# Smaller part tiles, and more products in pairs with a seven-product step, in a TensorE-bound decoder layer

## The chip, the cores and the metric

One core of one Trainium2 chip runs the whole layer. The metric is device time in microseconds (us), the median over several executions. Every matmul streams 512 columns of 32-bit data unless said otherwise.

## The reference

One hybrid decoder layer for 256 tokens of width 2048, in 32-bit floating point:

```
hn = rmsnorm(x);  q, k, v, g_ret, xr, yr, g_a, g_b = split(hn @ w_in)
ret_out = silu(g_ret) * groupnorm(retention(rotary(q), rotary(k), v))
rnn_out = gelu(yr) * rg_lru(causal_conv(xr))
merged  = sigmoid(g_a) * (ret_out @ w_proj_ret) + sigmoid(g_b) * (rnn_out @ w_proj_rnn)
h  = x + merged @ w_mix_out
h += cross_attention(rmsnorm(h), rmsnorm(mem))           # 256 memory tokens, 4 heads
up = causal_conv3(rmsnorm(h) @ ffn_w_up)                 # 2048 -> 2 * 5632
h += (silu(gate half of up) * value half) @ ffn_w_down
out = rmsnorm(h)
```

## The kernel before, in words

**Products.** An operand is kept as two parts, `hi` (rounded to the matmul's input format) and `lo` (what is left), and each product of two tiles is three matmuls: hi by hi, lo by hi, hi by lo. The activation side is stationary (128 x 128), the weight side streams (128 x 512). All large products are cut in column blocks of 512 (`BW`) and in k tiles of 128; the 256 tokens are two tiles of rows.

**Singles.** `gemm_n` (by `steps_n`) does one column block: it goes through its chunks of four k tiles (`KC`), and each chunk is 2 x 4 x 3 = 24 matmuls into one PSUM tile `acc` (three buffers of two banks).

**Pairs.** `pair` (by `steps_pair`) does two column blocks together. A chunk is a pair of k tiles (`KH`) of both blocks, also 24 matmuls, so a pair of 16 k tiles has eight chunks. At the k-pairs listed in `SEVEN` the four tile products of a 2 x 2 by 2 x 2 block product are replaced by Winograd's form with seven: 21 matmuls. It needs sums of the four weight tiles (four additions on the raw weights, L350), which are then split into parts like the weights themselves (`seven_parts`, seven part tiles instead of four), and sums of the activations (`sums_of`, kept in `token_sums`). It also needs four more PSUM banks, which are read into two SBUF tiles `o1`, `o2` after the last such k-pair (L495 to L502); at the pair's end four more additions (L513) bring in the other four banks.

**Weights.** `weight_plan` is the order of all products, `weight_stream` the order of their chunks in memory. A chunk of 1 MB is loaded to a `raw` tile (three buffers), ACT casts it to `hi` and the DVE subtracts to get `lo`. `prefetch` keeps two chunks prepared ahead of the one in use (`AHEAD = 2`); `hi` and `lo` have three buffers of 8 KB per partition (`PART_BUFS`).

**Order of the rest.** `chunks` counts a step after every chunk. `later(n, fn)` puts a piece of work into the program `n + 1` steps on. `by_dma` copies a result's 16-bit halves to planes on ACT (L535), transposes them by two DMAs on SP's queue (L536), and `wait + 1` steps later `join` puts them together on ACT (L548) and calls what follows. Every piece of work has its place in program order as its priority; an engine's queue is filled ahead of time from what is ready by an estimate, earlier place first, so a later piece can slip in while an earlier one isn't ready. The matmuls keep program order. Work in `high_priority(FREE)` is moved 300 places up. All tiles of 4 KB per partition share 29 buffers.

**The stages that the change touches**, in order: queries, keys, values and gates of retention (two groups of heads `g`), singles; `retain(g)` runs in small steps between the next products. Then the recurrence's blocks (singles), the gates `O_GB` (four singles), then `w_proj_rnn`, `O_GA` and `w_proj_ret`, two pairs each. In `w_mix_out` blocks 0 and 1 are a pair and blocks 2 and 3 singles; its left side `merged` is made by `turn_merged` from the joined results of `w_proj_ret`, block by block, two k-pairs from each. While it runs, `memory_steps` lets ACT take the squares of the rows of `mem` (L623), whose load is issued after the transposes. In the feed-forward, `ffn_w_up` runs as 22 singles, gate block and value block in turn; `conv_up` scales a result by the row norm on the DVE (L561), turns it by `by_dma` and applies three taps (L1107, L1109); after the value half `gate_up` forms `silu(gate) * value` (L1127 to L1129, L571, L572). After each of the first two parts of four blocks stands a `down` of two pairs, after the third `down_final`.

Of the kernel before, what the change touches and what calls it, by code (L numbers as in the profile page):

```python
# [17 lines left out]
P = 128  # L18
# [14 lines left out]
PART_BUFS = 3  # L33
# [9 lines left out]
SEVEN_O = (3, 5)  # L43

# [22 lines left out]

def weight_plan():

    plan = []  # L70
    for g in range(2):
        for c in (O_Q, O_K):
            plan += [("w_in", 0, NT, c + g * BW), ("w_in", 0, NT, O_V + g * 1024 + (c == O_K) * BW)]
        plan += [("w_in", 0, NT, O_G + g * 1024 + b * BW) for b in range(2)]
    for b in range(4):
        plan += [("w_in", 0, NT, c + b * BW) for c in (O_XR, O_YR)]
    plan += [("w_in", 0, NT, O_GB + b * BW) for b in range(4)]
    for w, c in (("w_proj_rnn", 0), ("w_in", O_GA), ("w_proj_ret", 0)):
        plan += [(w, 0, NT, (c + b * BW, c + (b + 1) * BW, SEVEN)) for b in (0, 2)]
    plan += [("w_mix_out", 0, NT, (0, BW, SEVEN))] + [("w_mix_out", 0, NT, b * BW) for b in (2, 3)]  # L80
    plan += [(w, 0, NT, b * BW) for b in range(4) for w in ("xa_w_k", "xa_w_q")]
    plan += [("xa_w_v", 0, NT, b * BW) for b in range(4)]
    plan += [("xa_w_o", 0, NT, (0, BW, SEVEN_O))] + [("xa_w_o", 0, NT, b * BW) for b in (2, 3)]
    for kind, *a in ff_plan():
        if kind == "down" and sum(a) < NF // 4:
            plan += [("ffn_w_down", a[0] * BW, 4 * a[1], (b * BW, (b + 1) * BW, SEVEN)) for b in (0, 2)]
        elif kind == "down":
            plan += [("ffn_w_down", a[0] * BW, 4 * a[1], b * BW) for b in range(4)]
        else:
            plan.append(("ffn_w_up", 0, NT, (0 if kind == "gate" else FF) + a[0] * BW))  # L90
    return plan
# [7 lines left out]
def ff_plan():  # L99

    out, b0 = [], 0
    for nb_ in FF_PARTS:
        ups = [(kind, b) for b in range(b0, b0 + nb_) for kind in ("gate", "value")]
# [47 lines left out]
def hybrid_layer(  # L151
# [104 lines left out]
    in_order = {sum(len(pieces(i, a[2], a[3])) for i, a in enumerate(plan[: gate_up_at() + 1])) + 1}  # L256

    def prefetch(n):
        while len(ahead) < n and taken[0] < len(stream):
# [56 lines left out]
            hi, lo = part_tiles()  # L316
            for k in range(0, nk, KH):
                if own:
                    xs[k2 + k // KH]
                if isinstance(c, tuple):  # L320
                    if k == 0:
                        weight_parts(raw, hi, lo)
                    continue
                for cs in (slice(k, k + 1), slice(k + 1, k + 2)) if i < 4 else (slice(k, k + KH),):
                    if i == 0 and cs.start == 0:
                        dve.tensor_copy(hi[:, cs], raw[:, cs, :])
                    else:
                        act.copy(hi[:, cs], raw[:, cs, :])  # L328
                    with tc.issue_after(split[cs.start]) if i == 0 else nullcontext():
                        dve.tensor_tensor(  # L330
                            out=lo[:, cs], in0=raw[:, cs, :], in1=hi[:, cs].bitcast(F32), op=ALU.subtract
                        )
            ahead.append(((row, c), (hi, lo)))

    def part_tiles():
        return [wp.tile([P, KC, BW], F32R, tag=a, bufs=PART_BUFS, name=nm(a)) for a in ("hi", "lo")]

    def weight_parts(src, hi, lo):

        act.copy(hi, src)  # L340
        dve.tensor_tensor(out=lo, in0=src, in1=hi.bitcast(F32), op=ALU.subtract)  # L341

    def seven_parts(raw):

        b12, b11, b22, b21 = (raw[:, i, :] for i in range(4))
        p_hi, p_lo = part_tiles()
        q_hi, q_lo = part_tiles()
        weight_parts(raw[:, 1:4], p_hi[:, 0:3], p_lo[:, 0:3])
        for o, a, b in ((b11, b12, b11), (b12, b12, b22), (b22, b11, b22), (b21, b22, b21)):
            dve.tensor_tensor(out=o, in0=a, in1=b, op=ALU.add)  # L350
        for c in (slice(0, 2), slice(2, 4)):
            weight_parts(raw[:, c], q_hi[:, c], q_lo[:, c])
        p1, p3, p2 = ((p_hi[:, i, :], p_lo[:, i, :]) for i in range(3))
        q3, q1, q2, q4 = ((q_hi[:, i, :], q_lo[:, i, :]) for i in range(4))
# [40 lines left out]
    def steps_n(w, row, st, nk, col):  # L395
# [3 lines left out]
        for k0, n, parts in chunks(nk, w, row, col):  # L399

            def tile_(tt, kk):
                k = k0 + kk
                hi, lo = (t[:, kk, :] for t in parts)
# [53 lines left out]
    def steps_pair(w, row, st, nk, c1, c2, seven=SEVEN):  # L457
# [14 lines left out]
        for k0, n, parts in chunks(nk, w, row, (c1, c2, seven)):  # L472
# [30 lines left out]
            else:  # L503
                end = k0 + n == nk
                for b, names in enumerate((("p2", "p4"), ("x3", "n"))):
                    hi, lo = (t[:, b * KH : (b + 1) * KH, :] for t in parts)
                    for tt, name in enumerate(names):
                        for j in range(KH):
                            rows_of(name, own[tt][j], (hi[:, j, :], lo[:, j, :]), end and j == KH - 1)
# [286 lines left out]
    for g in range(2):  # L796
        dec = big([P, 4, S], s="dec")
        vs, turned = [], ([], [])
        for b, o in enumerate((O_Q, O_K)):
# [12 lines left out]
            v = gemm_n("w_in", 0, xs, NT, O_V + g * 1024 + b * BW) if g + b else ended(v_steps)  # L812
            vs.append(split_rows(v, rs0))
        qr, kr = turned
        gates = []
        for b in range(2):
            a = gemm_n("w_in", 0, xs, NT, O_G + g * 1024 + b * BW)
# [3 lines left out]
            dve.scalar_tensor_tensor(out=t, in0=t, scalar=1.0, in1=a, op0=ALU.add, op1=ALU.mult)  # L821
            gates.append(t)
# [136 lines left out]
    ts = [tanh_rows(big([P, 2, BW], s="sig"), gemm_n("w_in", 0, xs, NT, O_GB + b * BW)) for b in range(4)]  # L959
    mb = []  # L960
    for b in (0, 2):
        for i, z in enumerate(pair("w_proj_rnn", 0, rnn, NT, b * BW, (b + 1) * BW)):
            gated(ts[b + i], z)
# [17 lines left out]
    def residual(w, st, out, wcol, steps=None):  # L981

        ss = sums()
        sources = []
        for b in range(4):
            if steps:
                steps(b)
            if not sources:
                if b == 0:
                    sources += pair(w, 0, st, NT, b * BW, (b + 1) * BW, SEVEN if steps else SEVEN_O)  # L990
                else:
                    sources.append(gemm_n(w, 0, st, NT, b * BW))
            h = hrow[b]
            dve.tensor_add(h, h, sources.pop(0))
# [119 lines left out]
    def conv_up(c0, b, dst, then):  # L1114


        def turned(f):
            conv(f, c0 // P + 4 * b, dst)
            then()

        turned_rows(gemm_n("ffn_w_up", 0, h2s, NT, c0 + b * BW), rs2, turned)

# [36 lines left out]
    def last_down(b0, hid, n, b):  # L1159
# [5 lines left out]
        parts = [p for _, _, p in chunks(n, "ffn_w_down", b0 * BW, b * BW)]  # L1165

        def total(o, tt, cs):
            for k in range(n):
                hi, lo = (t[:, k % KC, cs] for t in parts[k // KC])
# [50 lines left out]
    hid, gts = {}, {}  # L1220
    for kind, b, *n in ff_plan():
        if kind == "gate":
            gts[b] = big([P, 4, S], s="fg")
            conv_up(0, b, gts[b], lambda: None)
        elif kind == "value":
            vl = big([P, 4, S], s="fv")
            b0 = max(one[1] for one in ff_plan() if one[0] == "down" and one[1] <= b)
            seven = tuple(i - 2 * (b - b0) for i in SEVEN) if b0 < sum(FF_PARTS[:2]) else ()
            conv_up(FF, b, vl, lambda b=b, vl=vl, n=seven: gate_up(gts[b], vl, hid.setdefault(b, []), n))
# [50 lines left out]
```

## Time and profile before

| | before |
|---|---|
| median of 3 runs (lowest to highest) | 2017.43 us (2016.87 to 2017.99) |
| profiled execution | 2015.44 us |
| its span, first to last instruction | 2013.6 us |
| mean granted TensorE clock | 0.995 |
| TensorE matmul (PE) busy | 1985.5 us, 99% |
| VectorE (DVE) busy | 1450.8 us, 72% |
| ScalarE (ACT) busy | 1295.0 us, 64% |
| DMA | 425.54 MB, mean 211 GB/s |

In the profile's lines PE is TensorE's matmuls and PEld its weight loads, SPq is the queue of DMA issues on SyncE. A matmul's shown length is modelled and overlaps the next one's, so the pace is read from the starts. `x2` counts merged instructions; a bracket holds the engine's idle time before the instruction and what ended it. `acc` and `sm` are PSUM tiles, `s` and `ts` parts of activations and of their sums.

### The profile page before, as it was taken

Reading aid. Unit: us, or ns where it says so; the run is one execution under the profiler, and the core shown is the slowest. Engines: PE = TensorE matmul, PEld = TensorE weight load, DVE = VectorE, ACT = ScalarE, POOL = GpSimd, SP = SyncE. Lnnn points to the kernel's source line nnn. Section 1 sums busy time; section 2 is a strip of 40 time slices with the busy share of each in tenths; the row PEclk is TensorE's granted clock in tenths of the full one; section 3 lists DMA queues with packets and bytes.
Section 4 is the critical chain, followed back from the end, with each engine's and each line's share of the span. In section 5 each row is a group of like instructions: output and inputs, shape, how many; then the busy total and the mean of one; then the engine's idle time right before and its main releaser. Section 6 shows DMA issues by size and latency. Waiting matters only on the chain.

```text
span 2013.6 us, 23001 instructions
## 1 busy us (share of the span) xinstructions
PE 1985.5 (99%) x8882; PEld 1645.1 (82%) x8882; DVE 1450.8 (72%) x1781; ACT 1295.0 (64%) x1484; POOL 27.2 (1%) x25
## 2 busy tenths in 40 slices
PE   9999999999999999899999999999999999999998
PEld 8888887878888888678888888888888888888887
DVE  6857766898668988687555568677777777786775
ACT  7646547988544656578566666867764577744763
POOL 0000001000000000000000000000000000000000
PEclk9999999999999999999999999999999999999999
DMA  8755656665555455768567656766665667656673
GB/s 328 250 193 179 232 196 198 199 215 174 208 197 199 171 221 194 271 216 272 194 199 227 199 188 200 231 217 216 223 202 196 219 207 225 205 209 213 216 230 125
DMA packets 197181, 425.54 MB, mean 211 GB/s; under 512 B 142032, under 2 KB 146640, under 8 KB 152016
## 3 DMA queue, kind: packets, MB, share of 16 engines
q1 hardware_dynamic: 197072, 424.09, 62.9%
q8 instruction: 69, 1.13, 0.2%
q14 instruction: 40, 0.33, 0.0%
HBM read 388.39 MB, written 2.10 MB: 194 GB/s over the span
## 4 chain that ended last, share of the span: by engine, by line
PE 59%; issue 36%; ACT 2%; DVE 2%; DMA 1%; POOL 0%; SPq 0%; POOLq 0%; DVEq 0%; ACTq 0%
PE acc L236 51%; PE sm L236 8%; ACT hi L340 1%; DVE lo L341 1%; DMA nat<-in_mem 0%; ACT f L548 0%; ACT pl L535 0%; ACT hi L328 0%; DVE raw L350 0%; DVE lo L330 0%; DMA raw<-in_head 0%; DMA pt<-pl 0%; ACT rows L787 0%; DVE s L572 0%; ACT nat L623 0%
## 5 line engine op out<-in xcount | busy, mean ns | idle before, releaser
L236 PE MATMUL acc<-hi,s 128*128 128x512 f32 x4904 | 1508.6, 389 | 6.7 <-ACT s L571 4.6
L236 PEld LDWEIGHTS acc<-hi,s 128*128 128x128 f32 x4904 | 920.0, 188 | 197.2 <-ACT s L571 5.0
L236 PE MATMUL acc<-lo,s 128*128 128x512 f32 x2452 | 953.3, 389 | 2.0 <-DVE lo L341 1.7
L330 DVE TENSOR_TENSOR lo<-raw,hi 128x1024 fp32r<-128x1024 f32 (+1 forms) x524 | 621.0, 1216 | 281.8 <-ACT hi L328 281.0
L328 ACT CAST hi<-raw 128x1024 fp32r<-128x1024 f32 (+1 forms) x523 | 522.2, 1043 | 343.9 <-PE acc L236 226.6
L236 PEld LDWEIGHTS acc<-lo,s 128*128 128x128 f32 x2452 | 461.2, 188 | 99.7 <-DVE lo L341 3.9
L340 ACT CAST hi<-raw 128x2048 fp32r<-128x2048 f32 (+2 forms) x144 | 221.8, 1553 | 195.2 <-PE sm L236 72.0
L341 DVE TENSOR_TENSOR lo<-raw,hi 128x2048 fp32r<-128x2048 f32 (+2 forms) x144 | 262.3, 1844 | 91.5 <-ACT hi L340 91.3
L236 PE MATMUL sm<-hi,s 128*128 128x512 f32 x576 | 177.3, 389 | 0.0
L548 ACT COPY f<-pt 128x1024 uint16<-128x1024 uint16 x128 | 165.2, 1349 | 15.7 <-DMA pt<-pl 15.6
L236 PEld LDWEIGHTS sm<-hi,s 128*128 128x128 f32 x576 | 108.1, 188 | 22.5
L236 PE MATMUL sm<-lo,s 128*128 128x512 f32 x288 | 112.0, 389 | 0.0
L535 ACT COPY pl<-rows 128x1024 uint16<-128x1024 uint16 x100 | 99.4, 1043 | 14.8 <-DVE rows L559 9.0
L561 DVE TENSOR_SCALAR rows<-acc,ro 128x512 f32<-128x512 f32 x76 | 53.5, 745 | 39.0 <-PE acc L236 39.0
L350 DVE TENSOR_TENSOR raw<-raw 128x512 f32<-128x512 f32 x96 | 66.3, 691 | 2.7
L236 PEld LDWEIGHTS sm<-lo,s 128*128 128x128 f32 x288 | 54.1, 188 | 11.2
L1109 DVE SCALAR_TENSOR_TENSOR fv<-f,pf,fv 128x255 f32<-128x255 f32 (+1 forms) x88 | 37.6, 480 | 20.6 <-ACT fv L1107 20.3
L1109 DVE SCALAR_TENSOR_TENSOR fg<-f,pf,fg 128x255 f32<-128x255 f32 (+1 forms) x88 | 37.6, 480 | 16.6 <-ACT fg L1107 16.1
L236 PE MATMUL acc<-hi,ts 128*128 128x512 f32 x144 | 45.4, 397 | 1.9 <-ACT hi L340 1.8
L236 PEld LDWEIGHTS acc<-hi,ts 128*128 128x128 f32 x144 | 27.4, 192 | 8.3 <-ACT hi L340 2.8
L236 PE MATMUL acc<-lo,ts 128*128 128x512 f32 x72 | 29.1, 404 | 4.8 <-DVE lo L341 4.8
L569 DVE TENSOR_TENSOR s<-f,s 128x512 fp32r<-128x512 f32 x24 | 15.6, 688 | 15.8 <-ACT s L568 15.8
(190 smaller groups left out, 937.3 us busy)
## 6 DMA issues: line engine op xcount, KB each, us to landing
raw<-in_wall SPq DMA_DIRECT2D x352, 1024.0 KB, 4.8
nat<-in_x SPq DMA_DIRECT2D x8, 512.0 KB, 9.9
raw<-in_wall SPq DMA_DIRECT2D x7, 512.0 KB, 6.4
pt<-pl SPq DMA_TRANSPOSE x128, 3.2
nat<-in_mem SPq DMA_DIRECT2D x4, 512.0 KB, 10.0
xt<-in_x_t SPq DMA_DIRECT2D x3, 512.0 KB, 9.5
xt<-in_mem_t SPq DMA_DIRECT2D x3, 512.0 KB, 5.1
dec<-in_consts SPq DMA_DIRECT2D x2, 512.0 KB, 4.9
```

The lines of the kernel that those rows point to most:

```text
L236: tc.keep_in_program_order(pe.matmul(*a, **k))
L328: act.copy(hi[:, cs], raw[:, cs, :])
L330: dve.tensor_tensor(out=lo[:, cs], in0=raw[:, cs, :], in1=hi[:, cs].bitcast(F32), op=ALU.subtract)
L340: act.copy(hi, src)
L341: dve.tensor_tensor(out=lo, in0=src, in1=hi.bitcast(F32), op=ALU.subtract)
L350: dve.tensor_tensor(out=o, in0=a, in1=b, op=ALU.add)
L535: act.copy(planes[:, tt], words[:, tt])
L548: act.copy(halves_[:, :, :, cs], turned_[:, :, :, cs])
L561: dve.tensor_scalar_mul(rows[:, tt, :], a[:, tt, :], r[:, tt : tt + 1])
L569: dve.tensor_tensor(out=t[:, :, S:BW], in0=src, in1=t[:, :, 0:S].bitcast(F32), op=ALU.subtract)
L1109: dve.scalar_tensor_tensor(out=y[:, s:S], in0=z[:, j, 0 : S - s], scalar=pf[:, 2 - s, t : t + 1], in1=y[:, s:S], op0=ALU.mult, op1=ALU.add,)
```

## The change

**Part tiles.** `hi` and `lo` become tiles of two k tiles (4 KB per partition), six buffers each. A chunk takes two of each; a seven-product chunk takes four (one of them half used). Pair chunks are cast and subtracted in two instructions of 1024 columns instead of one of 2048. `parts` is now a list with one (hi, lo) for each k tile.

**New pairs, and one undone.** The values of the second group of heads, the gates `O_G` of both groups, and blocks 2 and 3 of `O_GB` run as pairs, each with two seven-product k-pairs (2, 5). The order there is: `O_GB` blocks 0 and 1 (singles), first pair of `w_proj_rnn`, `O_GB` blocks 2 and 3 (pair), second pair of `w_proj_rnn`. Blocks 0 and 1 of `w_mix_out` are no longer a pair: they are singles whose chunks run in turn, block 0's first three, block 1's first three, then the last of each. The last block of `merged` is joined with wait 3 instead of 2, and `merged` has no sums any more.

**The feed-forward.** Each of the 11 gate blocks runs as a pair with its value block, with one seven-product k-pair, number 4 (`SEVEN_U`). The scaling by the row norm moves to ACT, in place on the pair's result tiles; the gate half is joined with wait 1, the value half with wait 3.

The diff, cut to its core:

```diff
-PART_BUFS = 3
+PART_BUFS = 6
...
+SEVEN_U = (4,)
...
+def both(w, c, seven=SEVEN, row=0, nk=NT, apart=BW):
+    return w, row, nk, (c, c + apart, seven)
...
+        plan += keys + [both("w_in", O_V + 1024)] if g else [keys[0], values[0], keys[1], values[1]]
+        plan.append(both("w_in", O_G + g * 1024))
...
+    plan += [("w_in", 0, NT, O_GB + b * BW) for b in range(2)] + [both("w_proj_rnn", 0)]
+    plan += [both("w_in", O_GB + 1024), both("w_proj_rnn", 1024)]
+    plan += [both(w, c + b * BW) for w, c in (("w_in", O_GA), ("w_proj_ret", 0)) for b in (0, 2)]
+    plan += [("w_mix_out", 0, NT, b * BW) for b in range(4)]
...
+            plan.append(both("ffn_w_up", a[0] * BW, SEVEN_U, apart=FF))
...
+    i = [c[0][0] for c in out].index("w_mix_out")
+    out[i : i + 2] = [in_turn(out[i : i + 2])]
...
+    def weight_parts(src, pieces_=None):
+        n = src.shape[1]
+        hi, lo = (wp.tile([P, KH, BW], F32R, tag=a, bufs=PART_BUFS, name=nm(a)) for a in ("hi", "lo"))
+        for cs in pieces_ or (slice(0, n),):
+            act.copy(hi[:, cs], src[:, cs])
+            dve.tensor_tensor(out=lo[:, cs], in0=src[:, cs], in1=hi[:, cs].bitcast(F32), op=ALU.subtract)
+        return [(hi[:, i, :], lo[:, i, :]) for i in range(n)]
...
     def seven_parts(raw):
         b12, b11, b22, b21 = (raw[:, i, :] for i in range(4))
+        p1, p3 = weight_parts(raw[:, 1:3])
+        (p2,) = weight_parts(raw[:, 3:4])
         for o, a, b in ((b11, b12, b11), (b12, b12, b22), (b22, b11, b22), (b21, b22, b21)):
             dve.tensor_tensor(out=o, in0=a, in1=b, op=ALU.add)
+        q3, q1 = weight_parts(raw[:, 0:2])
+        q2, q4 = weight_parts(raw[:, 2:4])
         return [p1, p3, p2, q1, q3, q2, q4]
...
     def turn_merged(f):
         for pr in range(2):
-            with_sums(merged, SEVEN, f[:, 2 * pr : 2 * pr + 2, :], 0.5)
+            merged.append(split_pair(f[:, 2 * pr : 2 * pr + 2, :], 0.5))
...
-            by_dma(m, turn_merged, 1 + (b + i == 3))
+            by_dma(m, turn_merged, 1 + 2 * (b + i == 3))
...
+    def up(b, hid, seven):
+        gt, vl = (big([P, 4, S], s=a) for a in ("fg", "fv"))
+        def value(f):
+            conv(f, NF + 4 * b, vl)
+            gate_up(gt, vl, hid, seven)
+        two = pair("ffn_w_up", 0, h2s, NT, b * BW, FF + b * BW, SEVEN_U)
+        for a, then, wait in zip(two, (lambda f: conv(f, 4 * b, gt), value), (1, 3)):
+            with tc.high_priority(FREE):
+                for tt in range(2):
+                    act.mul(a[:, tt, :], a[:, tt, :], rs2[:, tt : tt + 1])
+            by_dma(a, then, wait)
```

More of the change, by code (lines that the diff above doesn't have):

```diff
@@ L102, in ff_plan @@
     for nb_ in FF_PARTS:
-        ups = [(kind, b) for b in range(b0, b0 + nb_) for kind in ("gate", "value")]
+        ups = [("up", b) for b in range(b0, b0 + nb_)]
         if b0:
@@ L319, in prefetch @@
                     xs[k2 + k // KH]
[L320 to L341, printed above, removed]
+                one = slice(k, k + KH)
+                if i == 0:
+                    parts += split_first(raw)
+                elif i < 4:
+                    parts += weight_parts(raw[:, one], (slice(0, 1), slice(1, 2)))
+                else:
+                    parts += weight_parts(raw[:, one])
@@ L983, in residual @@
         ss = sums()
+        products = [steps_n(w, 0, st, NT, b * BW) for b in range(4)]
         sources = []
```

93 lines of the change are left out of this document (43 added, 50 removed).

## The prediction

> **What bounds the kernel now.** I read the page's first part, then the waits of the PE, then the PE's timeline around one wait, then busy time by stretch, and last the groups by line and shape on the DVE. The first two fences are the page's first line and the waits.
>
> ```profile
> PE 1985.5 (99%) x8882; PEld 1645.1 (82%) x8882; DVE 1450.8 (72%) x1781; ACT 1295.0 (64%) x1484; POOL 27.2 (1%) x25
> ```
>
> ```profile
> PE acc L236 <- DVE lo L341: 6.5, 8, 1.8
> PE acc L236 <- ACT s L571: 4.6, 1, 4.6
> PE sm L236 <- ACT ti L876: 4.4, 1, 4.4
> PE acc L236 <- ACT hi L328: 1.9, 1, 1.9
> ```
>
> The PE works almost without a break, so the time is the number of matmuls times their pace, plus a handful of waits. The pace, and what a wait costs, stand in the PE's timeline (start, length, line, operation, idle before):
>
> ```profile
> 329.94 0.61 PE L236 MATMUL acc<-hi,s 128*128 128x512 f32 x2
> 330.62 0.61 PE L236 MATMUL acc<-hi,s 128*128 128x512 f32 x2
> 331.08 0.39 PE L236 MATMUL acc<-lo,s 128*128 128x512 f32 x1
> 333.40 1.03 PE L236 MATMUL acc<-hi,s 128*128 128x512 f32 x2 [1.93 <-ACT hi L328]
> 335.25 1.05 PE L236 MATMUL acc<-hi,s 128*128 128x512 f32 x2
> 336.11 0.63 PE L236 MATMUL acc<-lo,s 128*128 128x512 f32 x1
> ```
>
> From 329.94 to 330.62 three matmuls start: 0.2267 us each. After 331.08 the next start is at 333.40, 2.1 us late; then, from 335.25 to 336.11, two matmuls take 0.86 us, 0.43 each: the PE goes on at about half its pace for a while. So a wait of 2 us costs more than itself; I reckon up to some 1.6 us (eight matmuls at 0.2 us extra).
>
> Which engine could make the PE wait? Busy time by stretch (us, then PE, PEld, DVE, ACT, POOL; granted clock, DMA): the two pairs of the `O_GA` gates, the two pairs of `w_proj_ret`, the first pair of `w_mix_out`, and two gate and value blocks each of the feed-forward.
>
> ```profile
> 640.50:724.80 84.30, 84.30 (x374) 69.80 (x373) 79.08 (x95) 48.42 (x51) 0.00 (x0) 1.00 0.54 199
> 724.80:820.70 95.90, 93.92 (x412) 76.63 (x411) 79.92 (x76) 54.48 (x45) 0.00 (x0) 1.00 0.60 213
> 820.70:878.80 58.10, 47.85 (x191) 36.95 (x190) 40.62 (x44) 34.78 (x37) 2.85 (x1) 0.94 0.69 240
> 1357.40:1444.40 87.00, 87.00 (x385) 72.04 (x384) 64.95 (x91) 62.55 (x74) 0.00 (x0) 1.00 0.67 217
> ```
>
> The feed-forward's up product has the DVE at 75% and no PE wait at all. Where products run in pairs, the DVE is at 94% (gates, no wait) or 83% (`w_proj_ret`, 2.0 us of PE idle), and the first mix pair loses most: 191 matmuls by 0.2267 are 43.3 us, it took 58.1, so 14.8 us are lost.
>
> **The matmuls that go.** A k-pair done in seven products has 21 matmuls instead of 24. Before, 12 pairs have two such k-pairs each: 24. After: 2 each in the new V and G pairs (three of them) and in the new `O_GB` pair, none in `w_mix_out` any more (−2), and 1 in each of 11 up pairs: 24 + 8 − 2 + 11 = 41. Seventeen more, 51 matmuls fewer, by 0.2267 us: **−11.6 us**. Nothing else of the change can take PE work away.
>
> **The mix product.** Before, blocks 0 and 1 of `w_mix_out` are a pair; `merged[4]`, made from the third block of `w_proj_ret`, is first read in the fifth chunk. After, the two blocks run as singles in turn, and the third chunk already reads `merged[4]` (k 8 to 11). Timelines of SP, ACT and PE there:
>
> ```profile
> 827.59 4.01 SPq L536 DMA_TRANSPOSE pt<-pl  x3
> 835.41 3.35 SPq L207 DMA_DIRECT2D nat<-in_mem  x4
> 844.69 1.06 ACT L623 ACTIVATE nat<-nat 128x1024 f32<-128x1024 f32 x1 [7.75 <-DMA nat<-in_mem]
> 845.75 2.50 ACT L548 COPY f<-pt 128x1024 uint16<-128x1024 uint16 x2
> 821.37 0.61 PE L236 MATMUL acc<-hi,s 128*128 128x512 f32 x2
> 848.96 1.52 PE L236 MATMUL acc<-hi,s 128*128 128x512 f32 x2 [4.60 <-ACT s L571]
> ```
>
> The mix starts at 821.37. ACT stands 7.75 us before the squares of `mem`, whose load left SP only at 835.41, behind the transposes; the join of `merged[4]` (L548) is queued behind those squares, and the PE gets its operand at 848.96, 27.6 us after the start. The change moves none of these: the squares still fall due one chunk into the mix, the join (wait 1) two chunks in. What moves is the need: two chunks of 24 matmuls, 10.9 us after the start. The wait becomes 27.6 − 10.9 = 16.7 us, with the slow restart about 18.5, in place of the 14.8 lost now: **+4**. Fewer sums and parts around it on ACT and DVE don't bring the load of `mem` sooner. If the join gets ahead of the squares, the transposes (issued from 827.59) let it run near 833 and the wait is about 5 us: −10. I keep −10 to +5.
>
> **Part tiles of 4 KB.** Six halves instead of three wholes: a half is given back after half a pair's chunk, 12 matmuls or 2.7 us earlier, and a seven-product chunk takes four halves of six where it took two tiles of three. The 6.5 us of PE waits for L341 are all at such chunks, and the longest, in `w_proj_ret`, is this one:
>
> ```profile
> 809.45 0.50 PE L236 MATMUL acc<-lo,ts 128*128 128x512 f32 x1 [1.78 <-DVE lo L341]
> ```
>
> I take that wait as gone, **−2**, range −4 (nearly all that lies outside the mix) to +2. The price is two instructions of 1024 in place of one of 2048 (first fence: the DVE's groups in 1357.4 to 1444.4, two gate and value blocks; second: groups of the whole span):
>
> ```profile
> L330 DVE TENSOR_TENSOR lo<-raw,hi 128x1024 fp32r<-128x1024 f32 x32 | 38.1, 1220 | 10.4 <-ACT hi L328 10.4
> L561 DVE TENSOR_SCALAR rows<-acc,ro 128x512 f32<-128x512 f32 x8 | 5.6, 745 | 5.5 <-PE acc L236 5.5
> L1109 DVE SCALAR_TENSOR_TENSOR fv<-f,pf,fv 128x255 f32<-128x255 f32 x8 | 3.7, 481 | 3.4 <-ACT fv L1107 3.4
> L1109 DVE SCALAR_TENSOR_TENSOR fv<-f,pf,fv 128x254 f32<-128x254 f32 x8 | 3.7, 480 | 0.1
> L572 DVE SCALAR_TENSOR_TENSOR s<-fo,s 128x512 fp32r<-128x512 f32 x4 | 2.8, 688 | 0.0
> L1129 DVE TENSOR_TENSOR fo<-fo,fv 128x512 f32<-128x512 f32 x4 | 2.8, 688 | 0.0
> L1128 DVE SCALAR_TENSOR_TENSOR fo<-ft,fg 128x512 f32<-128x512 f32 x4 | 2.7, 684 | 0.0
> ```
>
> ```profile
> L341 DVE TENSOR_TENSOR lo<-raw,hi 128x2048 fp32r<-128x2048 f32 x72 | 163.6, 2289 | 76.5 <-ACT hi L340 76.3
> L350 DVE TENSOR_TENSOR raw<-raw 128x512 f32<-128x512 f32 x96 | 66.3, 691 | 2.7
> L513 DVE TENSOR_TENSOR o<-o,sm 128x512 f32<-128x512 f32 x24 | 15.5, 680 | 0.0
> ```
>
> 2 × 1.22 − 2.29 is 0.15 us a chunk on an engine that has room there.
>
> **The up products, the large term.** Per gate and value block the DVE is busy 64.95 / 2 = 32.5 us of 43.5 now. The seven-product chunk adds one subtraction of 1024 (38.1/32 = 1.19 us), one of 512 (0.69) and four additions (66.3/96 = 0.69 each): 4.6 us. The pair's results leave PSUM in eight additions (15.5/24 = 0.65 each, 5.2) instead of four scalings (5.6 for two blocks, 2.8): +2.4. That is 39.5 us in 189 × 0.2267 = 42.8 us, 92%. ACT gains 1.5 casts, a copy and four scalings on 31.3 us; at the DVE's lengths for such tiles (1.19 and 0.69) that is 5.0 us, 85%. On the sum both still fit. In order they don't: the value half of a block now comes through its join four chunks into the next pair, ahead in the queue of the parts of chunk 6, and the seven-product chunk is chunk 4. What the DVE must do from the parts of chunk 4 (its lookahead of two chunks lets it begin when the PE begins chunk 2) to those of chunk 6: the gate's taps 3.7, the parts of chunk 4 3 × 1.19 + 0.69 + 4 × 0.69 = 7.0, chunks 5 and 6 4 × 1.19 = 4.8, the value's taps 3.7, four additions out of PSUM 2.6, and `gate_up` 8.3 / 2 = 4.1: 25.9 us. The PE's chunks 2 to 5 last 93 × 0.2267 = 21.1 us. The DVE comes up to 4.8 us late for chunk 6; if the gate's taps are done before, 1.1. Singles had the same taps without the 7.0 and the 2.6, and no wait.
>
> The nearest rows are the gates (94%, no wait, but small steps spread over the chunks) and `w_proj_ret` (83%, with bursts, 2.0 us idle). The up pairs have bursts, so I take 2.2 us in each place. Places: up pairs that follow an up pair (eight of 11) and the first down pair after up 4 and after up 8 (two): ten, **+22**, range 0 to +45 with slow restarts at the upper end.
>
> The Trainium skill, "TensorE: Matmul & The Clock Gate" (section "Why this matters for your kernels"), allows idle gaps of up to about 3 us before the clock falls; by it waits of 2.2 us cost only themselves, and the sum stays as it stands. The rows above, half pace after a gap of 2.3 us, speak for more.
>
> **New pairs in retention and merge.** Each adds 2 × 4.6 us for its two chunks and 5.2 for eight additions to the DVE; with 16 subtractions (19.0) that is 33 of 42.2 us, and the values' splits, the gates' product and K's rotation come on top. The gates at 94% without a wait are the nearest row, yet two pairs stand in a row there: **+2**, range 0 to +6. The order of `O_GB` and `w_proj_rnn` costs nothing: the last `rnn` pairs are due seven chunks after their product and read fourteen after it; if that cover went, ACT's chain of a few us would show.
>
> **The sum.** −11.6 + 4 − 2 + 22 + 2 = +14.4. The profiled execution took 2015.44 us (span 2013.6 and 1.8 around it): 2029.8. The median of the runs, 2017.43, is 2.0 above the profiled one; 2017.43 + 14.4 gives **2032 us**.
>
> **Rivals.** (1) *Two chunks of lookahead cover the bursts.* Nothing waits in the up pairs, as in the gates: −11.6 + 4 − 2 + 1 = −8.6, 2009 us; with the join ahead of the squares, 1995. For it: the sums of busy time fit, and 94% went without a wait. Against it: in `w_proj_ret` 83% with bursts did not. (2) *The mix wait goes, the up waits stay*: 14 lower, 2018, no change to be seen; it hangs on whether the `mem` load lands before `merged[4]` needs ACT. (3) *Slower by more*: the full 4.8 us and slow restarts in ten places, or result and plane tiles of two blocks at once short of the 29 shared buffers: 2055 and above. The point from which (1) turns into my forecast: 8.6 us over ten places, 0.9 us each.
>
> **How the numbers follow.** Forecast 0.50, (1) 0.22, (2) 0.16, (3) 0.12. The lower end takes in the slower half of (1), 2006; the upper end most of the forecast's range and the beginning of (3), 2054. A measurement here tells about 0.2%, 4 us, from no change. Slower: the forecast, (3) and a little of (2), 0.68; same: 0.11, from (2) and the weak edge of the forecast; faster: (1), 0.21.
>
> **What would show it.** Right: 8831 matmuls; in the PE's waits a new large row for `lo` or `hi` of the parts, near the seventh chunk of the up pairs; DVE over 90% in them; one PE wait of 15 to 18 us in the mix before an ACT split. Wrong: no PE wait in the up pairs and a span under 2010; or a mix wait of 5 us.

## The result, and the profile after

The changed kernel takes **2011.37 us** (median of 7 runs, 2009.85 to 2013.18) against 2017.43 of the kernel before in the same comparison: ratio 0.9975, 95% interval 0.9965 to 0.9985. It is 6 us faster, where 15 us slower was forecast. The profiled execution took 2011.37 us, with a span of 2009.4 us.

The first line of the page of after, and its PE waits (who waited for whom; us in total, times, longest):

```profile
PE 1971.7 (98%) x8831; PEld 1635.7 (81%) x8831; DVE 1564.5 (78%) x2044; ACT 1370.1 (68%) x1671; POOL 25.4 (1%) x25
```

```profile
PE acc L245 <- ACT s L582: 17.1, 1, 17.1
PE sm L245 <- ACT ti L890: 8.1, 2, 6.6
PE acc L245 <- DVE lo L344: 2.8, 4, 1.0
PE acc L245 <- ACT hi L343: 1.4, 1, 1.4
```

The 51 matmuls are gone, and the DVE has 114 us more to do. One wait for a split (`s`, the mix) and the recurrence's `ti` hold most of the idle time; no row for `lo` or `hi` has grown as the forecast had it. Busy time by stretch of after (us, then PE, PEld, DVE, ACT, POOL; granted clock, DMA): the mix, and two stretches of 43 us of the up pairs.

```profile
817.00:880.00 63.00, 45.86 (x192) 37.20 (x191) 29.34 (x30) 33.52 (x40) 0.70 (x1) 0.86 0.69 226
1345.00:1388.00 43.00, 43.00 (x191) 35.65 (x190) 36.80 (x53) 34.80 (x44) 0.00 (x0) 1.00 0.68 217
1388.00:1431.00 43.00, 43.00 (x191) 35.60 (x191) 37.25 (x56) 34.22 (x44) 0.00 (x0) 1.00 0.58 203
```

In these two stretches of up pairs the PE has no idle time at all, and the DVE stands at 86 and 87%, not 92%. No wait there, with a span under 2010 us, is what the prediction gave as its sign of being wrong.

To see where the time went, I add up from the starts of the matmuls what each came later than the usual spacing (0.227 us for 512 columns, 0.119 for 256). This "lost" time holds waits and slow restarts alike, in us:

| stage | before | part tiles alone | after | best version |
|---|---|---|---|---|
| start, first group of retention (to 150 us) | 1.1 | 0.9 | 1.8 | 1.4 |
| second group of retention (150 to 300) | 0.7 | 0.8 | 5.8 | 0.7 |
| recurrence (300 to 560) | 11.7 | 4.3 | 10.6 | 3.9 |
| gates, `w_proj_ret` (560 to 815) | 2.9 | 0 | 0 | 0 |
| mix (815 to 905) | 15.0 | 12.3 | 19.8 | 0.9 |
| attention (905 to 1310) | 0.4 | 0 | 0 | 0 |
| feed-forward (from 1310) | 1.3 | 0.6 | 2.8 | 6.3 |
| sum | 33.1 | 18.9 | 40.8 | 13.2 |

From before to after that is 7.7 − 51 × 0.2267 = −3.9 us, and the spans differ by −4.2: the table accounts for the change, as these two profiled executions show it (the medians differ by 6.1). Its columns two and four are experiments, told below: before_halves and late_two_two.

### The profile page after: what moved, and what is told of

The parts are those of the page before. It is cut to its first block, busy times and chain, and to the rows that moved or that the text cites. A ratio compares the mean times of both kernels' runs of the same rounds, so it can differ in the third digit from the quotient of the medians.

```text
span 2009.4 us, 24019 instructions
## 1 busy us (share of the span) xinstructions
PE 1971.7 (98%) x8831; PEld 1635.7 (81%) x8831; DVE 1564.5 (78%) x2044; ACT 1370.1 (68%) x1671; POOL 25.4 (1%) x25
## 4 chain that ended last, share of the span: by engine, by line
PE 92%; DVE 3%; ACT 2%; issue 1%; DMA 1%; SPq 0%; POOL 0%; POOLq 0%; DVEq 0%; ACTq 0%
PE acc L245 67%; PE sm L245 25%; DVE lo L344 1%; ACT hi L343 1%; ACT f L559 0%; DMA nat<-in_mem 0%; ACT pl L546 0%; DVE tb L728 0%; DVE xr L925 0%; PE warm L242 0%; DVE rows L572 0%; DMA pt<-pl 0%; DVE ta L732 0%; DVE raw L364 0%; DVE fv L1127 0%
## 5 line engine op out<-in xcount | busy, mean ns | idle before, releaser
L245 PE MATMUL acc<-hi,s 128*128 128x512 f32 (+1 forms) x3974 | 1221.9, 389 | 17.2 <-ACT s L582 17.1
L344 DVE TENSOR_TENSOR lo<-raw,hi 128x1024 fp32r<-128x1024 f32 (+1 forms) x796 | 933.4, 1197 | 337.2 <-ACT hi L343 328.4
L343 ACT CAST hi<-raw 128x1024 fp32r<-128x1024 f32 (+1 forms) x796 | 792.4, 1023 | 419.0 <-PE acc L245 145.5
L245 PEld LDWEIGHTS acc<-hi,s 128*128 128x128 f32 x3974 | 745.5, 188 | 170.5 <-ACT s L582 17.6
L245 PE MATMUL acc<-lo,s 128*128 128x512 f32 (+1 forms) x1987 | 772.1, 389 | 1.7 <-DVE lo L344 1.7
L245 PEld LDWEIGHTS acc<-lo,s 128*128 128x128 f32 x1987 | 374.1, 188 | 79.4 <-DVE lo L344 2.5
L245 PE MATMUL sm<-hi,s 128*128 128x512 f32 x1336 | 411.3, 389 | 0.0
L245 PEld LDWEIGHTS sm<-hi,s 128*128 128x128 f32 x1336 | 250.8, 188 | 52.0
L245 PE MATMUL sm<-lo,s 128*128 128x512 f32 x668 | 260.0, 389 | 0.0
L245 PEld LDWEIGHTS sm<-lo,s 128*128 128x128 f32 x668 | 125.4, 188 | 26.0
L245 PEld LDWEIGHTS acc<-hi,ts 128*128 128x128 f32 x246 | 46.3, 189 | 11.7 <-ACT hi L343 2.2
```

Source lines behind the costliest of these rows:

```text
L245: tc.keep_in_program_order(pe.matmul(*a, **k))
L343: act.copy(hi[:, cs], src[:, cs])
L344: dve.tensor_tensor(out=lo[:, cs], in0=src[:, cs], in1=hi[:, cs].bitcast(F32), op=ALU.subtract)
```

## The experiments

The kernel before ran beside each group of experiments (medians 2015.1, 2016.6, 2016.2 and 2016.9 us); ratios are to those runs. Those medians and the 2017.43 of the result differ among themselves by 2.3 us, so a difference between an experiment and the changed kernel, 2011.37, is good to about 2 us.

| kernel | median us | ratio, 95% interval | lost us |
|---|---|---|---|
| up_singles | 2018.41 | 1.0010, 1.0001 to 1.0019 | 40.0 |
| two_sevens_up | 2021.41 | 1.0031, 1.0019 to 1.0044 | 59.2 |
| up_load_1 | 2020.25 | 1.0016, 1.0007 to 1.0025 | 51.0 |
| up_load_3 | 2071.58 | 1.0276, 1.0262 to 1.0290 | 105.5 |
| up_load_3_late | 2060.60 | 1.0216, 1.0202 to 1.0230 | 89.4 |
| value_wait_1 | 2041.31 | 1.0128, 1.0113 to 1.0143 | 69.6 |
| before_halves | 2002.08 | 0.9930, 0.9918 to 0.9943 | 18.9 |
| vg_singles | 2012.30 | 0.9977, 0.9968 to 0.9987 | 36.9 |
| all_vg_singles | 2005.50 | 0.9947, 0.9934 to 0.9959 | 30.5 |
| buffers_30 | 2005.70 | 0.9942, 0.9928 to 0.9955 | 34.6 |
| late_squares | 1997.15 | 0.9907, 0.9892 to 0.9922 | 26.6 |
| mix_pair | 2005.15 | 0.9949, 0.9936 to 0.9961 | 37.3 |
| late_mix_pair | 2003.29 | 0.9933, 0.9921 to 0.9945 | 34.7 |
| late_three | 1999.02 | 0.9914, 0.9900 to 0.9927 | 29.1 |
| late_all_vg | 1994.08 | 0.9886, 0.9873 to 0.9900 | 19.1 |
| late_two_two | 1987.36 | 0.9853, 0.9840 to 0.9867 | 13.2 |

**The up pairs: is there a cover, and how thick is it?** The theory after the result: the DVE's queue in the up pairs is as the prediction described it, but its work is less, and the parts of chunk 6 are ready shortly ahead of their need. The rival: it has room to spare.

up_singles undoes the up pairs alone:

```
-            plan.append(both("ffn_w_up", a[0] * BW, SEVEN_U, apart=FF))
+            plan.append(("ffn_w_up", 0, NT, (0 if kind == "gate" else FF) + a[0] * BW))
...
```

> The feed-forward's up product is put back to 22 singles (gate and value in turn, waits 1 and 1, scaling on the DVE), all else as after the change. The prediction's reading (up pairs cost some 22 us of PE waits): this kernel is faster than the changed one by 22 - 7.5 = 14 us, about 1997 us. The rival (the lookahead covers the bursts; the changed kernel's trace shows no PE wait in the up pairs): it has 33 matmuls more, 33 x 0.2267 = 7.5 us, and nothing else, about 2019 us.

It took 2018.41, 7.0 us above the changed kernel; the 33 matmuls are worth 7.5, and the feed-forward loses 2.2 us here against 2.8 in the changed kernel. So the up pairs bring just about what their matmuls are worth, and everything else of the change together comes out 0.1% behind the kernel before.

two_sevens_up does two k-pairs in seven products in place of one:

```
-SEVEN_U = (4,)
+SEVEN_U = (2, 5)
```

> The up pairs get seven-product chunks at k-pairs 2 and 5 instead of 4 alone: 33 matmuls fewer, 7.5 us. Theory A (the DVE keeps up because in a full queue its instructions follow each other at 0.61 us for 512 columns and 1.14 us for 1024, which leaves it about 38 of 42.9 us busy in an up pair, a margin of a few us): the second chunk adds 1.14 + 0.61 + 4 x 0.61 = 4.2 us, 42.3 of 42.2 us, so the margin is gone and the PE waits in most up pairs, 1 to 3 us each: 2015 to 2035 us. Theory B (later parts slip into the gaps whatever the load, and the PE's two chunks of lookahead are ample): no waits, 2011.4 - 7.5 = 2004 us.

It took 2021.41, in theory A's range: 33 more matmuls are gone, and 17.7 us more are lost in the feed-forward (20.5 against 2.8). One stretch of 43 us of its up pairs:

```profile
1431.00:1474.00 43.00, 39.57 (x170) 31.33 (x170) 40.47 (x59) 34.17 (x43) 0.00 (x0) 1.00 0.68 222
```

The DVE stands at 94% here and the PE waits. A second seven does not fit.

up_load_1 and up_load_3 add DVE work that nobody reads, two or six multiplications of 128x512 in each up pair:

```
+            for _ in range(1):   # range(3) in up_load_3
+                dve.tensor_tensor(out=th, in0=gt[:, cs, :], in1=vl[:, cs, :], op=ALU.mult)
             dve.tensor_tensor(out=o, in0=o, in1=vl[:, cs, :], op=ALU.mult)
```

> As the kernel with six more multiplications, but two in each up pair, 1.2 us by 0.61. Theory of a margin of 1 us: +0 to +6, 2011 to 2017, few waits in the up pairs. Rival, with ample gaps: +0, 2011. If it loses 10 us or more, the margin was smaller than the one place that was looked at showed.

> Leaves nothing out: six more multiplications of 128x512 on the DVE in each of the 11 up pairs (three in each half of gate_up), whose results nobody reads; at the pace seen in full queues, 0.61 us from start to start, that is 3.7 us a pair. It brings the DVE's work to what the prediction had reckoned by lengths of single instructions. Theory (the prediction's queue was right in kind, and only the sizes were too large: parts of chunk 6 were ready about 1 us ahead of their need): the cover is gone, 2.7 us late in ten places, +20 to +45, 2031 to 2056, with PE waits on lo or hi near the seventh chunk. Rival (the parts slip into gaps between dependent steps, and the DVE still has 3 us free in each pair): no more than +5, 2011 to 2016.

Two cost 8.9 us over 11 pairs, more than the 6 I gave as the most; six cost 60 us, well above the 45. The cover is thinner than 1.2 us in some of the pairs: nearly all that up_load_1 loses more stands in up 3 and up 8 (blocks counted from 0) and in the down pairs after up 4 and up 8. With 3.7 us more a pair loses 5.5 on average, more than the added work. The two largest `lo` rows of the PE waits of up_load_3, and its DVE and PE timelines (start, length, engine, line) around the longest:

```profile
PE acc L245 <- DVE lo L344: 31.0, 16, 6.8
...
PE sm L245 <- DVE lo L344: 10.5, 4, 3.5
```

```profile
1413.82 0.68 DVE L1139 TENSOR_TENSOR ft<-fg,fv 128x512 f32<-128x512 f32 x1
...
1421.18 0.68 DVE L583 SCALAR_TENSOR_TENSOR s<-fo,s 128x512 fp32r<-128x512 f32 x1
1421.78 0.68 DVE L514 TENSOR_TENSOR o<-o,acc 128x512 f32<-128x512 f32 x1
1422.38 1.21 DVE L344 TENSOR_TENSOR lo<-raw,hi 128x1024 fp32r<-128x1024 f32 x1
```

```profile
1423.65 0.79 PE L245 MATMUL acc<-lo,s 128*128 128x512 f32 x1 [6.84 <-DVE lo L344]
```

From 1413.82 to 1422.38 the DVE works without a pause on `gate_up`, its sums and the first addition out of PSUM, and no L344 stands between them; the subtraction behind them releases the PE. This is the very queue that the prediction described, here with 3.7 us more in it. Compare after, at the same place of the same pair, up 2 (its DVE timeline, then its PE timeline):

```profile
1390.65 1.23 DVE L344 TENSOR_TENSOR lo<-raw,hi 128x1024 fp32r<-128x1024 f32 x1 [1.78 <-ACT hi L343]
...
1406.26 0.68 DVE L1138 TENSOR_TENSOR fo<-fo,fv 128x512 f32<-128x512 f32 x1
1406.87 1.21 DVE L344 TENSOR_TENSOR lo<-raw,hi 128x1024 fp32r<-128x1024 f32 x1
1408.00 0.68 DVE L583 SCALAR_TENSOR_TENSOR s<-fo,s 128x512 fp32r<-128x512 f32 x1
1408.61 0.41 DVE L448 TENSOR_TENSOR tq<-fo 128x256 f32<-128x256 f32 x1
1408.94 1.21 DVE L344 TENSOR_TENSOR lo<-raw,hi 128x1024 fp32r<-128x1024 f32 x1
```

```profile
1411.16 0.61 PE L245 MATMUL acc<-hi,s 128*128 128x512 f32 x2
1411.62 0.39 PE L245 MATMUL acc<-lo,s 128*128 128x512 f32 x1
```

Both subtractions of chunk 6 stand between the steps of `gate_up`, where it has to wait for ACT. The second ends at 1408.94 + 1.21 = 1410.15, and the PE begins chunk 6 at 1411.16, 1.0 us later. The cover is larger than that: the chunk's first matmul with a `lo` reads the first of the two, which ended at 1408.08, and starts at 1411.62, 3.5 us later; the second belongs to the other column block, which the PE reaches 12 matmuls further on.

Counted in this way, the first part of chunk 6 is ready 3.5, 3.5, 1.2, 0.4, 4.2, 2.2, 0.4 and 3.6 us ahead in the eight up pairs that follow an up pair. From the first subtraction for chunk 4 to the first for chunk 6 the DVE takes 17.4 to 18.0 us in all eight; it begins later the more up pairs stand in a row (0.0, 0.6, 2.3 and 3.6 us after the PE begins chunk 2 in up 1 to up 4). In the first down pair after up 4 and after up 8 the PE does wait at chunk 6, 0.7 and 1.0 us: these two of the prediction's ten places have a wait.

value_wait_1 leaves the work alone and changes only where the value's burst falls, one chunk into the next pair in place of three:

```
-        for a, then, wait in zip(two, (lambda f: conv(f, 4 * b, gt), value), (1, 3)):
+        for a, then, wait in zip(two, (lambda f: conv(f, 4 * b, gt), value), (1, 1)):
```

> The changed kernel with the value half's join, taps and gate_up due one chunk after the pair, as the gate half's, in place of three: both bursts then fall ahead of the seven-product chunk's parts, and one transposition more stands at once on the queues. Theory (a margin of about 1 us decides, and order with it): the burst piles up with the gate's taps and the seven's 7 us of parts; 3 to 6 us of waits in ten places, 2030 to 2070. Rival (the DVE catches up, since it has 7 us free in each pair and the parts slip in between): within 4 us of the changed kernel, 2008 to 2016.

2041.31: 28.6 us more are lost in the feed-forward with the same DVE work. The PE's waits for `lo` are 15.7 us (2.8 in the changed kernel) and those for ACT's `hi` 7.4 (1.4). So the place of this work in the queues, ACT's among them, decides some 30 us.

up_load_3_late moves the loaded burst two chunks later, behind the parts of chunks 6 and 7:

```
-        for a, then, wait in zip(two, (lambda f: conv(f, 4 * b, gt), value), (1, 3)):
+        for a, then, wait in zip(two, (lambda f: conv(f, 4 * b, gt), value), (1, 5 if b < 10 else 3)):
```

> The kernel with six more DVE multiplications in each up pair (2071.6), and the value half's join, taps and gate_up due two chunks later, behind the parts of chunks 6 and 7 (in all up pairs but the last). The DVE's work for a pair stays what it was, about 39 of 42.8 us by starts. Theory (the order of the queue decides: the loss comes where the value's burst stands ahead of the parts of chunks 6 and 7): most of the 60 us goes, 2015 to 2040. Rival (the DVE's sum of work decides, with what the casts make it wait): the loss only moves to later chunks, 2055 to 2090.

2060.60: the rival's range. Of the 60 us only 11 go; with the DVE this full (37 + 3.7 of 42.8 us, 95%), the loss turns up elsewhere, most of it at the first chunk of the pair that follows. So neither order nor sum decides alone: at 86% the order does (value_wait_1), at 95% the order tried here saved little.

**Part tiles alone.** before_halves is the kernel before with the part tiles of 4 KB, the new `weight_parts` and `seven_parts`, and nothing else:

```
-PART_BUFS = 3
+PART_BUFS = 6
...
-        return [wp.tile([P, KC, BW], F32R, tag=a, bufs=PART_BUFS, name=nm(a)) for a in ("hi", "lo")]
+        hi, lo = (wp.tile([P, KH, BW], F32R, tag=a, bufs=PART_BUFS, name=nm(a)) for a in ("hi", "lo"))
...
```

> The kernel before with the part tiles of 4 KB alone: six halves in place of three wholes, and the parts of a seven-product chunk in four instructions of one or two k-blocks. No matmul changes. By the prediction's term of -2, with the 2.9 us lost in w_proj_ret gone, 2 to 4 us faster than before: 2012 to 2015. Rival (more instructions on a DVE at 83%, and the same number of bytes): no change, 2015 to 2018.

2002.08, 14 us faster than before: more than the whole change brings. Its PE waits:

```profile
PE acc L236 <- ACT s L573: 6.1, 1, 6.1
PE sm L236 <- ACT ti L878: 3.4, 3, 1.6
PE acc L236 <- ACT hi L334: 1.2, 1, 1.2
```

The 2.9 us of `w_proj_ret` go as foreseen. The larger part goes in the recurrence, 11.7 to 4.3, whose two waits the prediction had shown but not counted. In before, 4.2 of the 11.7 stand at the wait for ACT's cast at 333.40 and 7.3 at the wait for `ti` at 443.94. The PE's row there, then ACT's timeline of before and of before_halves ahead of the same `ti`:

```profile
443.94 2.93 PE L236 MATMUL sm<-rp,rp 128*128 128x256 f32 x12 [4.42 <-ACT ti L876]
```

```profile
439.63 1.99 ACT L535 COPY pl<-rows 128x1024 uint16<-128x1024 uint16 x2 [1.19 <-DVE rows L561]
441.53 1.99 ACT L328 CAST hi<-raw 128x1024 fp32r<-128x1024 f32 x2
443.43 0.83 ACT L876 ACTIVATE ti<-sm,h 128x256 f32<-128x256 f32 x2
```

```profile
432.03 1.03 ACT L334 CAST hi<-raw 128x1024 fp32r<-128x1024 f32 x1
432.97 1.99 ACT L537 COPY pl<-rows 128x1024 uint16<-128x1024 uint16 x2
434.86 0.83 ACT L877 ACTIVATE tr<-sm,h 128x256 f32<-128x256 f32 x2
435.59 1.04 ACT L334 CAST hi<-raw 128x1024 fp32r<-128x1024 f32 x1
436.52 0.84 ACT L878 ACTIVATE ti<-sm,h 128x256 f32<-128x256 f32 x2
```

Before, a pair of casts stands in front of `ti`; with halves one of them is done ahead of the plane copies. I read from this that a half tile comes free earlier and the casts spread out; the run shows the gain, not which of these casts made it, nor how much of it the four instructions of a seven-product chunk have.

**Retention and the shared buffers.** vg_singles undoes the two new pairs of the second group:

```
+        plan += [keys[0], values[0], keys[1], values[1]]
+        plan += [("w_in", 0, NT, O_G + 1024 + b * BW) for b in range(2)] if g else [both("w_in", O_G)]
...
```

> The second group's values and gates in retention as single products again. Twelve matmuls come back, +2.7 us. Theory (the two pairs in a row crowd the DVE and ACT, which the 5.1 us of waits near 199 and 215 to 222 us show): these waits go, -5.1, in sum -2.4: about 2009. Rival (the waits come from what else is queued there, K's rotation and the retention scores, and come back in another place): +2.7 or more, 2014 and above.

2012.30 against 2011.37, no difference that counts, and between the two expectations. The waits went as expected (5.8 to 0.9), the 12 matmuls came back, and the feed-forward lost 1.1 more. As a pair or as singles, this comes to the same. But the recurrence still lost 10.8, and ACT and SP of after show why (ACT, then SP):

```profile
485.02 1.98 ACT L546 COPY pl<-rows 128x1024 uint16<-128x1024 uint16 x2
486.91 1.99 ACT L343 CAST hi<-raw 128x1024 fp32r<-128x1024 f32 x2
491.60 0.84 ACT L890 ACTIVATE ti<-sm,h 128x256 f32<-128x256 f32 x2 [2.71 <-DMA pt<-pl]
```

```profile
487.03 2.61 SPq L547 DMA_TRANSPOSE pt<-pl  x2
```

`ti` reads nothing of that transposition. It waits for the buffer that the transposed plane gives back: one of the 29 shared ones. The first pair of retention needs the token sums of x. In after they are made at 103 and 108 us, in before only at 656 and 662, for the gates of the merge; from then on they hold two of the 29. Two runs tell this from other reasons. all_vg_singles makes, beyond vg_singles, the first group's gates single too, and buffers_30 keeps all pairs and pays for one more shared buffer with a temporary:

```
-        plan.append(both("w_in", O_G + g * 1024))
+        plan += [("w_in", 0, NT, O_G + g * 1024 + b * BW) for b in range(2)]
...
```

```
-    bp = ctx.enter_context(tc.tile_pool(name="bp", bufs=29))
-    tp = ctx.enter_context(tc.tile_pool(name="tp", bufs=10))
+    bp = ctx.enter_context(tc.tile_pool(name="bp", bufs=30))
+    tp = ctx.enter_context(tc.tile_pool(name="tp", bufs=9))
```

> The changed kernel with all values and gates of retention as single products, the first group's gates too. Eighteen matmuls come back, +4.1 us. With no pair in retention the token sums of x are first made for the O_GB pair near 650 us instead of at 103 us, and hold two of the 29 shared buffers for 550 us less. Theory (these two buffers are what the recurrence lacks: ti waits 4.7 us for a transposed plane to come free at 486.9): the 6.8 us wait at 485 falls to below 2, and the 5 us near 199 and 215 to 222 go: 4.1 - 11 = -7, about 2004.5. Rival (the recurrence waits for another reason; with the second group's pairs alone undone the wait stayed 6.35): only the 5 go, 2010 to 2013.

> The changed kernel with 30 shared buffers in place of 29, paid for by 9 in place of 10 small temporaries. Theory (a shared buffer is short in the recurrence): the 6.8 us wait at 485 gets shorter by 4 to 6.5, 2005 to 2008. Rival (no shortage; or the ninth temporary is missed elsewhere): 2011 or more.

2005.50 and 2005.70: both by the theory, 6 us each. In the PE waits of buffers_30 the row of `ti` reads

```profile
PE sm L245 <- ACT ti L890: 2.6, 2, 1.5
```

in place of 8.1 and 6.6. A single shared buffer was short.

**The mix.** The forecast's wait is there, in after's PE timeline:

```profile
828.09 0.39 PE L245 MATMUL acc<-lo,s 128*128 128x512 f32 x1
845.62 1.52 PE L245 MATMUL acc<-hi,s 128*128 128x512 f32 x2 [17.14 <-ACT s L582]
```

late_squares takes the squares of `mem` out of the way of the join, by four chunks:

```
-                later(c, lambda c=c: sum_squares(mnat[c], ss, c))
-            later(4, lambda: rsms.append(rstd_rows(ss)))
+                later(4 + c, lambda c=c: sum_squares(mnat[c], ss, c))
+            later(8, lambda: rsms.append(rstd_rows(ss)))
```

> The four squares of the rows of mem fall due four chunks later in the mix product, and their row norm too; nothing else changes. Theory (the 17 us wait of the PE at the third mix chunk is the join of merged[4] queued on ACT behind squares that wait for the load of mem): the join runs as soon as its transposes have landed, the wait becomes 3 to 6 us, the whole 11 to 15 us faster than the changed kernel, 1997 to 2000 us. Rival (the join itself lacks its transposes or a free buffer until then): the wait stays at 15 us or more, 2009 to 2012 us.

1997.15, 14.2 us below the changed kernel, and the wait is

```profile
PE acc L245 <- ACT s L582: 4.0, 1, 4.0
```

So ACT's queue, with squares that wait for a load, made 13 us of the 17. mix_pair makes the first two blocks of `w_mix_out` a pair again:

```
-    plan += [("w_mix_out", 0, NT, b * BW) for b in range(4)]
+    plan += [both("w_mix_out", 0)] + [("w_mix_out", 0, NT, b * BW) for b in (2, 3)]
...
```

> Blocks 0 and 1 of w_mix_out are a pair again with two seven-product chunks, merged has its sums and the last block's join its wait of 2; all else as after the change. Theory (the in-turn singles need merged[4] two chunks earlier, and so wait longer for the same landing of mem): the loss in the mix goes from 19.8 back to about 15 us and 6 matmuls (1.4 us) go: 5 to 6 us faster than the changed kernel, about 2005.5 us. Rival (the loss in the mix is about the same in either form): 1.4 us faster, 2010 us.

2005.15, 6.2 us below: 6.5 us less are lost in the mix (19.8 to 13.3) and 6 matmuls go, 1.4; some 3 us come back in the recurrence and the feed-forward (the spans differ by 4.6). Both together, late_mix_pair:

> The changed kernel with the squares of mem due four chunks later and the first two blocks of w_mix_out as a pair again. The later squares alone gave 1997.2, the pair alone 2005.2. Theory (the pair reads merged[4] two chunks later than the singles in turn, so that nothing of the wait is left when the join is not behind the squares): of the 6.4 us lost in the mix with late squares 4 to 6.4 go, and two more sevens take 1.4: 1989 to 1992. Rival (the pair's parts and sums at the place where the squares now fall, ACT and DVE both busy, cost as much as the wait): 1996 to 2000.

2003.29. It misses both ranges: the pair reads `merged[4]` in time now, but a cast for raw weights is late (4.7 us) and the mix still loses 10.5. late_three tried three blocks in turn:

```
-    out[i : i + 2] = [in_turn(out[i : i + 2])]
+    out[i : i + 3] = [in_turn(out[i : i + 3])]
...
```

> The kernel with the squares of mem four chunks later (1997.2), and three blocks of w_mix_out in turn in place of two, so that merged[4] is needed after two chunks of each of three blocks, 72 matmuls or 16.3 us after the start, in place of 10.9; mem's own transposition is set one product earlier to stay where it was. Theory (the 6.4 us that are left there are operand time against need): the need is 5.4 us later, the wait of 4.2 and its slow restart go, 1990 to 1993. Rival (a weight load or a cast is late there next, as in the kernel with both late squares and the pair, where a cast for raw weights was 4.8 us late): 1995 to 2000.

1999.02, and the wait is the 4.0 us of late_squares. The expectation misread the order: in turn means three chunks of the first block, then three of the second, so that `merged[4]` is read in the first block's third chunk whatever the number of blocks. late_two_two does it right, on top of late_all_vg (all retention products single, late squares): two chunks of each block, then one of each, then one.

```
-    out[i : i + 2] = [in_turn(out[i : i + 2])]
+    one, two = out[i : i + 2]
+    out[i : i + 2] = [one[:2] + two[:2] + one[2:3] + two[2:3] + one[3:] + two[3:]]
...
```

> All values and gates of retention single, and the squares of mem four chunks later. By the sum of the two effects (-7 and -14.2): 1990. If either takes the other's place: 1995 to 1998.

> As the kernel before it in this list, and the first two blocks of w_mix_out in turn by two chunks, then one, then one: both blocks' first two chunks come ahead of the first use of merged[4], which is needed 96 matmuls or 21.8 us after the start in place of 10.9. Theory (the 6.4 us left in the mix with late squares are merged[4]'s wait): they go, about 1984. Rival (the next late thing is a weight load there, as raw weights that landed only at 847 with late squares, some 20 us after the start): half of it comes back, 1987 to 1990.

late_all_vg took 1994.08, 4 us short of the sum of both effects; why is open. late_two_two took away the whole mix loss, 6.9 to 0.9: the wait was `merged[4]`'s need. Its 1984 was reckoned from the 1990 that late_all_vg missed; from 1994.08 it is 6.7 us less, as its theory has it. The feed-forward loses 6.3 here against 2.8 in the changed kernel; no run shows why. It took **1987.36 us**, 1.5% below the kernel before and 24 us below the changed one. The PE waits of late_two_two have no `s` row any more:

```profile
PE acc L246 <- DVE lo L345: 4.9, 6, 1.7
PE sm L246 <- ACT ti L888: 2.9, 3, 1.6
```

## Why the prediction was wrong

In the table's columns the change goes: part tiles −14.2; then −51 matmuls −11.6, mix +7.5, second group +5.0, recurrence +6.3, feed-forward +2.2, start +0.9. Together −3.9.

- **The matmuls that go, −11.6**: right, 8831 run now, 51 fewer.
- **The up products, +22: the step that failed**, and with it the sign. The measured price is about 0.6 us in the feed-forward (2.8 lost against 2.2 with singles), not 22, and the pairs bring 7.0 us. The queue was there (value_wait_1 and up_load_3 show it at work), but the burst ahead of chunk 6 was reckoned too large: 25.9 us, and in up 2 it took 19.5, from 1390.65 to 1410.15.
  - *Sizes*, about 2 of the 6.4 us. The working added up lengths of single instructions, 0.69 for 128x512 and 1.22 for 128x1024. In a full queue they start 0.61 and 1.14 apart (1406.26 to 1406.87, 1406.87 to 1408.00 above), so that a whole pair has some 37 us of DVE work, not 39.5.
  - *Order*, about 4.5. The working put all of the value burst and the four additions out of PSUM ahead of the parts of chunk 6, where the order in the program has them. In the trace half of `gate_up` stands behind ACT, the subtractions are placed into those gaps, and the additions come after them.
  - *The need*. Both parts of chunk 6 were taken as due when the chunk begins; the PE reads the second 12 matmuls, 2.7 us, later.
  - Together this turned 1.1 to 4.8 us late into 0.4 to 4.2 us early in the eight up pairs. The prediction had named the point from which its rival wins, 0.9 us a place.
- **Rival (1)** is what the up pairs did, and its 2009 us is near the result, but that is luck: −2 for part tiles and +1 for the new pairs should have been −14 and +11, and the two errors nearly cancel.
- **Part tiles, −2**: alone they bring 14. The step looked for waits at seven-product chunks alone. Half of the gain lies in the recurrence, at a late cast and at a `ti` that stood behind casts on ACT; the prediction quoted both rows (`hi` L328 and `ti` L876) and did not use them.
- **The mix, +4**: right in mechanism and size, 19.8 lost against 15.0; the wait was forecast at 16.7 and was 17.1.
- **New pairs in retention and merge, +2**: 5.0 in place, and 6.3 more in the recurrence by the shared buffers that the token sums hold. The prediction did bring up the 29 buffers, but only for the up pairs.

The starts of a full queue could be read in the trace of before, in which the instruction after this one of length 1.22 starts 1.14 us behind it:

```profile
1415.66 1.22 DVE L330 TENSOR_TENSOR lo<-raw,hi 128x1024 fp32r<-128x1024 f32 x1
1416.80 1.29 DVE L1128 SCALAR_TENSOR_TENSOR fo<-ft,fg 128x512 f32<-128x512 f32 x2
```

## What to carry to other kernels

Cost a burst on a busy engine by its starts in a full queue, not by the lengths of its instructions, and compare the order in which the trace shows them, not the order of the program; ask of each operand at which matmul it is first read; where the answer turns on a few microseconds a place, give both signs like chances. When a product moves earlier, look at what it makes and how long that now stays in shared memory: the wait shows up hundreds of microseconds later, at an instruction whose data has nothing to do with it. Part of a change measured alone can be worth more than the whole.

## What the runs showed of the hardware

How long a wait may be before the PE restarts slowly came out sharper than the prediction's rows had it. Two waits of the PE timeline of up_load_3_late:

```profile
1753.13 0.50 PE L245 MATMUL acc<-lo,s 128*128 128x512 f32 x1 [1.76 <-DVE lo L344]
1753.47 0.64 PE L245 MATMUL acc<-hi,s 128*128 128x512 f32 x2
1753.94 0.40 PE L245 MATMUL acc<-lo,s 128*128 128x512 f32 x1
1754.18 0.62 PE L245 MATMUL acc<-hi,s 128*128 128x512 f32 x2
...
1851.23 0.77 PE L245 MATMUL sm<-lo,s 128*128 128x512 f32 x1 [2.08 <-DVE lo L344]
1851.79 1.05 PE L245 MATMUL sm<-hi,s 128*128 128x512 f32 x2
1852.65 0.63 PE L245 MATMUL sm<-lo,s 128*128 128x512 f32 x1
1853.07 1.05 PE L245 MATMUL sm<-hi,s 128*128 128x512 f32 x2
```

After the first (which starts 1.93 us later than usual) three matmuls take 0.71 us, from 1753.47 to 1754.18: the usual pace. After the second (2.24 late) three take 1.28, from 1851.79 to 1853.07, some 0.43 each. The granted clock in the 3.4 us from each of the two waits on is 1.00 and 0.51. In all runs here, gaps of up to 1.9 us with no other shortly before them were followed by ten matmuls of 512 columns at 0.24 to 0.26 us, and gaps from 2.2 us on by ten at 0.32 to 0.47, whether 2.2 or 18 us long; between 1.9 and 2.2 us there are too few to say where the limit lies. So a slow restart costs 1 to 2.5 us (ten times 0.1 to 0.25), once. The Trainium skill, "TensorE: Matmul & The Clock Gate" (section "Why this matters for your kernels"), allows gaps of up to about 3 us; these runs put the limit near 2.
